# First seven-product block two blocks later, activation sums spread out, conditioning regrouped

## The chip, the core and the metric

The kernel runs on one core of one Trainium2 chip. The engines of the core work side by side and meet only at semaphores: TensorE (PE: matrix products, with PEld for loading the stationary operand), VectorE (DVE), ScalarE (ACT), GpSimd (POOL) and SyncE (SP, which here issues most transfers). Operands lie in on-chip memory in 128 partitions; products are summed in PSUM. The metric is the device time of one launch in microseconds. Before the change three runs took 3255.46, 3265.27 and 3267.32 us; the median, 3265.27 us, is the time to which the change is compared.

## The reference

The input is one sequence of 512 positions with 1024 features. It goes through three layers: two "first" layers (l = 0, 1) and one "second" layer. Each has a feed-forward part (FFN), a mixer (four kinds of attention or recurrence) and another FFN, so there are six FFNs. In the first layers each part is conditioned on a vector `c`:

```python
cond = jax.nn.silu(c)
mod = (cond @ ada_w[l] + ada_b[l]).reshape(B, N_SUBLAYERS, 3, 1, D)   # per part: shift, gain, gate
h = adaln_pre(x, norm_g[l, 0], mod[:, 0, 0], mod[:, 0, 1])            # rms norm, times (1+gain), plus shift
x = x + 0.5 * mod[:, 0, 2] * swiglu(h, ffn1_w13[l], ffn1_w2[l])
def swiglu(h, w13, w2):
    a, b = jnp.split(h @ w13, 2, axis=-1)
    return (jax.nn.silu(a) * b) @ w2                                   # 1024 -> 2816 -> 1024
```

The second layer's FFNs have the same form without conditioning.

## The kernel before

**Precision.** Every matrix product is made of three: a float32 value is split into a high part `hi` (a cast by ACT) and a low part `lo` (value minus `hi`, by DVE), and PE sums hi·hi, hi·lo and lo·hi (`mm3`, lines 308, 311 and 312; line 889 in the seven-product blocks). So each half chunk of weights costs one ACT cast (line 786) and one DVE subtraction (line 787) before PE can use it.

**An FFN** (`ffn`, line 827) makes the 2816 hidden features in 22 blocks (n = 0 to 21) of 128, each with a gate half (`a`) and an up half (`b`). A block is made in one of two ways:

- *plain* (`Q`, `unit_q`): four units of 12 matmuls with 512 columns, 48 in all.
- *seven-product* (`P`, `unit_p`): seven units of 12 matmuls with 256 columns, 84 in all. This form replaces eight half-size products by seven. It needs four sums of weight quarters per block (tiles `S`, line 769, DVE), and sums of activations that are the same for all blocks of the FFN (tiles `e`, made once by `tsums`, line 797).

The units of P are numbered 1, 2, 5, 6, 3, 7 and 4; 1 and 2 (PSUM tiles `A` and `B`) and 3 use the plain activations `hh`, `hl`; the third in order, 5 (PSUM tile `D`), is the first to need a sum of weights and the `e` tiles. Unit 4 of a block is put into the block after it. Which blocks are P is set by the tuple `seven`: twelve blocks from n = 3 in the four FFNs of the first layers, nine odd ones from n = 3 in the two FFNs of the second layer (there `norm` is set). After blocks 6, 14 and 21 the hidden features made so far are multiplied down to the output (units `D`, 16 per slab, the "slabs").

`Units` (line 697) lists all units in order and works five ahead: `take` hands one unit to PE, after `ahead` has loaded, cast and subtracted until five are ready. Hence the order of the program on each engine is the order in which this code issues work; each engine then runs its own list strictly in order, and a scheduler only interleaves neighbours.

**tsums** works in four steps (k = 0 to 3). In each, DVE scales two feature blocks (line 2116), forms four half-width sums and differences (lines 807 and 809) and, after two ACT casts, two low parts (line 824). `ffn` calls one step after each of the units 1 to 4 (`next(ts)`), and `first_block()` after unit 0.

**Conditioning.** 16 modulation vectors of 1024 are made in the background of the FFNs and of the mixers' last product. For each, eight weight chunks of 512 KB are loaded by SP (`ada_load`, line 380), DVE adds chunk times condition to an accumulator `acc` (lines 396 and 398), and then PE transposes `acc` (line 406, eight matmuls) and DVE reduces it to a vector (line 407). `ada_ahead` issues a load if none is waiting in `ada_in`; `bg` runs one step of `mod_steps`. In an FFN the calls stand in alternating units (plain units, the down units, and P blocks with n divisible by 4). Inside an FFN the chunk's tile has one buffer (`bufs=1`).

**Small results.** `snap` copies 128x256 pieces of PSUM to tiles `sn` (five buffers, ACT, line 899); the sum of two of them goes to a tile `c` (line 920, DVE), used in line 924.

**Side work.** `side` is a generator that sets up tables for the mixers, one step after each finished block with n > 2. In the first FFN its first step loads a table on POOL's queue into one of the four weight buffers (line 525), its second multiplies it on PE (line 533).

The lines of the program that the diff touches:

Of the kernel before, what the change touches and what calls it, by code (L numbers as in the profile page):

```python
# [9 lines left out]
F32 = mybir.dt.float32  # L10
F32R = mybir.dt.float32r
AF = mybir.ActivationFunctionType
ALU = mybir.AluOpType
# [6 lines left out]
KD = 8  # L20
# [205 lines left out]
def _body(tc, nc, ctx, I, out):  # L226
# [10 lines left out]
    def nm(s):  # L237
        cnt[0] += 1
        return f"{s}{cnt[0]}"
# [139 lines left out]

    def ada_load(pool):  # L380
        l, k, c0 = ada_src.pop(0)
        raw = pool.tile([128, 1024], F32, tag="raw", bufs=4 if pool is WB else 1, name=nm("raw"))
        nc.sync.dma_start(raw, I["ada"][l, k * 128:(k + 1) * 128, c0:c0 + 1024])
        return raw

    def ada_ahead(pool):

        if ada_src and not ada_in:
            ada_in.append(ada_load(pool))

    def mod_steps(l, s, r):
        acc = P.tile([128, 1024], F32, tag="acc", bufs=1, name=nm("acc"))
        for k in range(KD):
            raw = ada_in.pop(0) if ada_in else ada_load(WB)
            if k == 0:
                i = V.tensor_scalar(acc, raw, cond[:, 0:1], None, op0=ALU.mult)
            else:
                i = V.scalar_tensor_tensor(acc, raw, cond[:, k:k + 1], acc, op0=ALU.mult, op1=ALU.add)  # L398
            dep(i, order["lo"])
            if k < KD - 1:  # L400
                yield
        m = P.tile([128, KD], F32, name=nm("mod"))
        for g in range(2):
            ps = psa()
            for k in range(4):
                PE.transpose(ps[:, k * 128:k * 128 + 128], acc[:, (4 * g + k) * 128:(4 * g + k) * 128 + 128], ident)
            V.tensor_reduce(m[:, 4 * g:4 * g + 4], ps.rearrange("p (k c) -> p k c", k=4), axis=AX.X, op=ALU.add)
        V.tensor_tensor(m, m, C(("adab", l), (3 * s + r) * 8, 8), op=ALU.add)
        if r == 1:
            V.scalar_tensor_tensor(m, m, 1.0, C(("ng", l), s * 8, 8), op0=ALU.add, op1=ALU.mult)  # L410
        elif r == 2 and s != 1:
            V.tensor_scalar(m, m, 0.5, None, op0=ALU.mult)
        mods[l, s, r] = m
        yield

    def all_steps():
        for m in MODS:
# [88 lines left out]
    def bg():  # L506
        next(bg_it, None)
# [319 lines left out]
    def ffn(wa, wd, emit_d, q0=None, side=None, norm=None, operand=None):  # L827
# [3 lines left out]
            yield  # L831
            yield from fr
        table(SILU_SET)
        seven = (3, 5, 7, 9, 11, 13, 15, 17, 19) if norm is not None else (3, 4, 5, 7, 8, 10, 11, 13, 15, 16, 18, 19)
        with tc.tile_pool(name=nm("fp"), bufs=1) as FP:
            f = Units(wa, wd, FP, seven)
            e = [FP.tile([128, 4, 4, 256], F32R, name=nm("e")) for _ in range(2)]
# [40 lines left out]
            def unit_p(n, p, w):  # L878
                S_ = f.acc.setdefault(n, {})
                b = {1: "A", 6: "A", 7: "A", 4: "A", 2: "B", 5: "D", 3: "D"}[p]  # L880
                if p in (1, 2, 5):
                    S_[b] = (psm if b == "B" else psa)(b)
                q = S_[b][:, 0:256]
                k0, t = {1: (0, 0), 2: (4, 0), 3: (4, 1)}.get(p, (None, {5: 0, 6: 1, 7: 2, 4: 3}.get(p)))
                for k in range(4):
                    s = slice(k * 128, k * 128 + 128)
                    xh, xl = (a[:, k, t] if k0 is None else a[:, k0 + k, HV[t]] for a in (e if k0 is None else (hh, hl)))
                    for i, (v, x) in enumerate(((w[0], xh), (w[0], xl), (w[1], xh))):
                        PE.matmul(q, v[:, s], x, start=p in (1, 2, 5) and k + i == 0, stop=k == 3 and i == 2,  # L889
                                  skip_group_check=p not in (1, 2, 5))  # L890

                if n % 4 == 0 and p == 1:
                    ada_ahead(FP)
                elif n % 4 == 0 and p == 3:
                    bg()

                def snap(i):
                    S_[i] = FP.tile([128, 256], F32, tag="sn", bufs=5, name=nm("sn"))
                    S.copy(S_[i], q)
                if p == 1:  # L900
                    snap(1)
                elif p == 2:
                    S_["g"] = FP.tile([128, 512], F32, tag="ga", bufs=2, name=nm("ga"))
                    V.tensor_tensor(S_["g"][:, HV[0]], S_[1], q, op=ALU.add)
                elif p == 5:
                    snap(5)
                elif p == 6:
                    snap(2)
                elif p == 3:
                    g = S_["g"]  # L910
                    V.tensor_tensor(g[:, HV[1]], S_[2], q, op=ALU.add)
                    if norm is not None:
                        V.tensor_tensor(g, g, box["r"], op=ALU.mult)
                    act(g, g, AF.Silu)
                    if norm is not None:
                        V.tensor_tensor(g, g, box["r"], op=ALU.mult)
                elif p == 7:
                    snap(3)
                    S_["c"] = FP.tile([128, 256], F32, tag="c", bufs=2, name=nm("c"))
                    V.tensor_tensor(S_["c"], S_[3], S_[5], op=ALU.add)  # L920
                else:
                    u, g = w_("u"), S_["g"]
                    V.tensor_tensor(u[:, HV[0]], g[:, HV[0]], q, op=ALU.mult)
                    V.tensor_tensor(u[:, HV[1]], g[:, HV[1]], S_["c"], op=ALU.mult)
                    hidden(n, u)
                    del f.acc[n]

# [14 lines left out]
            while f.n[1] < len(f.units):  # L942
                x = f.units[f.n[1]]
                if x[0] == "D" and x[1] == 2 and x[2] == KD - 2:
                    break
                x, w = f.take()
                if x[0] == "D":
                    s, d, h = x[1:]
                    slab, m = SLABS[s], len(SLABS[s]) // 2
                    if (s, d, h) == (2, 0, 0):  # L950
                        table(LN_SET)
                    if h == 0:
                        qd[d] = psa() if d % 2 else psm()
                    mm(qd[d], w, slab[h * m:h * m + m], ALL, h * m, 2 * m)
                    if h:
                        bg()
                    else:
                        ada_ahead(FP)
                    if h and s < 2:
                        emit_d.acc(d, qd[d], s == 0)  # L960
                    elif h:
                        emit_d(d, qd[d], ALL, False)
                else:
                    (unit_q if x[0] == "Q" else unit_p)(x[1], x[2], w)
                if done == 0:
                    first_block()
                elif done < 5:
                    next(ts)
                done += 1
            if ada_in:  # L970
                bg()
            qs, ws = {}, {}
            for d in (KD - 2, KD - 1):
# [1205 lines left out]
```

## Time and profile before

| | before |
|---|---|
| median of three runs | 3265.27 us |
| the profiled execution | 3260.05 us |
| its span, first to last instruction | 3258.3 us |
| mean granted TensorE clock | 0.986 of full |
| PE busy | 3150.6 us (97%) |
| DVE busy | 2228.9 us (68%) |
| ACT busy | 1517.7 us (47%) |
| chain that ended last | PE 83%, DVE 9%, DMA 2%, ACT 2% |

The profile is of one execution. Its busy shares are means over the whole span; a view with a window shows a stretch of it. On PE "idle before" is time in which the engine waited, with the instruction that released it. Matmuls overlap: the distance between the starts of two of them, not the duration of one, is what a matmul costs in a row of many. The four FFNs of the first layers begin their block 1 near 60, 792, 1161 and 1886 us of the span; the two of the second layer lie after 2230 us.

### The profile page before, as it was taken

The page shows a single profiled execution, that of the slowest core. Times are in us where ns is not written, and L with a number is a line of the kernel's source. Part 1 is how long each engine was busy: PE and PEld are TensorE (multiplying, and loading weights), DVE is VectorE, ACT ScalarE, POOL GpSimd, SP SyncE. Part 2 cuts the span into 40 slices and gives each one's busy share as a digit, 9 for nine tenths or more (in the row PEclk, how much of TensorE's full clock was granted, in tenths as well). Part 3 has the DMA queues.
Part 4 walks back from the last instruction along what each step waited for, and adds up shares of the span by engine and source line. Part 5 has one row for each costly group of instructions (what it writes and reads, how often), then busy time and mean ns, then how long its engine had stood idle before and what let it go on. Part 6 is the DMA issues. An engine that isn't in the chain of part 4 may idle for free.

```text
span 3258.3 us, 49205 instructions
## 1 busy us (share of the span) xinstructions
PE 3150.6 (97%) x18436; PEld 2753.0 (84%) x18436; DVE 2228.9 (68%) x4084; ACT 1517.7 (47%) x2953; POOL 422.2 (13%) x492
## 2 busy tenths in 40 slices
PE   7999999999999999999999999999999999999998
PEld 5898877888898888898788898888888788888887
DVE  7787676668887697775766686567566544576664
ACT  4453354553453353343555554345444445664442
POOL 2000132213000210003221311002000210220001
PEclk8999999999999999999999999999999999999999
DMA  6545542114555535543320334234332355433322
GB/s 226 172 155 170 183 136 85 40 50 152 170 160 162 162 112 180 174 151 124 105 75 30 110 101 159 90 123 141 98 110 98 114 171 151 133 122 112 104 96 92
DMA packets 136287, 415.38 MB, mean 127 GB/s; under 512 B 16824, under 2 KB 31036, under 8 KB 135776
## 3 DMA queue, kind: packets, MB, share of 16 engines
q1 hardware_dynamic: 129840, 391.27, 37.6%
q0 software_dynamic: 6064, 20.76, 2.1%
q8 instruction: 145, 2.38, 0.3%
q14 instruction: 94, 0.77, 0.1%
q10 hardware_dynamic: 144, 0.21, 0.0%
HBM read 379.58 MB, written 22.51 MB: 123 GB/s over the span
## 4 chain that ended last, share of the span: by engine, by line
PE 83%; DVE 9%; DMA 2%; ACT 2%; POOL 2%; issue 2%; SPq 0%; DVEq 0%; ACTq 0%; POOLq 0%
PE A L889 11%; PE m L311 10%; PE m L308 10%; PE m L312 10%; PE a L308 7%; PE a L311 7%; PE a L312 7%; PE D L889 6%; PE B L889 3%; PE o L1655 2%; PE pt L1649 1%; DMA raw<-in_ada_dram 1%; DVE lo L297 1%; DVE acc L398 1%; DVE lo L787 1%
## 5 line engine op out<-in xcount | busy, mean ns | idle before, releaser
L786 ACT CAST hi<-raw 128x512 fp32r<-128x512 f32 (+1 forms) x726 | 438.5, 607 | 713.4 <-PE m L311 289.4
L787 DVE TENSOR_TENSOR lo<-raw,hi 128x512 fp32r<-128x512 f32 (+1 forms) x726 | 486.6, 675 | 226.9 <-ACT hi L786 217.1
L308 PE MATMUL m<-hh,hi 128*128 128x512 f32 (+1 forms) x1200 | 467.8, 390 | 11.4 <-ACT hh L483 6.4
L311 PE MATMUL m<-hl,hi 128*128 128x512 f32 (+1 forms) x1200 | 461.4, 385 | 10.6 <-DVE hl L638 8.3
L312 PE MATMUL m<-hh,lo 128*128 128x512 f32 (+1 forms) x1200 | 457.5, 381 | 5.0 <-DVE lo L297 5.0
L889 PE MATMUL A<-e,hi 128*128 128x256 f32 x1584 | 295.7, 285 | 0.1
L297 DVE TENSOR_TENSOR lo<-raw,hi 128x512 fp32r<-128x512 f32 (+1 forms) x264 | 200.2, 769 | 136.9 <-ACT hi L296 129.0
L786 ACT CAST hi<-S 128x512 fp32r<-128x512 f32 x264 | 163.8, 622 | 269.8 <-PE a L311 113.3
L308 PEld LDWEIGHTS m<-hh,hi 128*128 128x128 f32 x1200 | 230.9, 192 | 51.8 <-ACT hh L483 6.5
L311 PEld LDWEIGHTS m<-hl,hi 128*128 128x128 f32 x1200 | 230.7, 192 | 50.7 <-DVE hl L638 10.8
L311 PE MATMUL a<-hl,hi 128*128 128x512 f32 (+1 forms) x736 | 270.4, 367 | 2.4 <-DVE hl L628 2.4
L312 PEld LDWEIGHTS m<-hh,lo 128*128 128x128 f32 x1200 | 230.5, 192 | 47.5 <-DVE lo L297 7.6
L308 PE MATMUL a<-hh,hi 128*128 128x512 f32 (+1 forms) x736 | 269.6, 367 | 0.0
L312 PE MATMUL a<-hh,lo 128*128 128x512 f32 (+1 forms) x736 | 269.1, 366 | 0.0
L296 ACT CAST hi<-raw 128x512 fp32r<-128x512 f32 (+1 forms) x264 | 158.4, 614 | 237.1 <-PE m L311 124.8
L889 PEld LDWEIGHTS A<-e,hi 128*128 128x128 f32 x1584 | 252.1, 194 | 3.9 <-ACT hi L786 0.7
L787 DVE TENSOR_TENSOR lo<-S,hi 128x512 fp32r<-128x512 f32 x264 | 181.1, 688 | 76.5 <-ACT hi L786 76.0
L889 PE MATMUL A<-e,lo 128*128 128x256 f32 x792 | 225.3, 285 | 0.0
L308 PE MATMUL m<-u,hi 128*128 128x512 f32 (+1 forms) x576 | 216.0, 375 | 0.0
L308 PE MATMUL a<-u,hi 128*128 128x512 f32 (+1 forms) x576 | 215.1, 374 | 0.0
L311 PE MATMUL a<-u,hi 128*128 128x512 f32 (+1 forms) x576 | 214.4, 372 | 0.0
L312 PE MATMUL a<-u,lo 128*128 128x512 f32 (+1 forms) x576 | 214.4, 372 | 0.0
(524 smaller groups left out, 7124.5 us busy)
## 6 DMA issues: line engine op xcount, KB each, us to landing
raw<-in_ada_dram SPq DMA_DIRECT2D x144, 512.0 KB, 4.1
raw<-in_f1a_dram SPq DMA_DIRECT2D x88, 512.0 KB, 4.3
raw<-in_f2a_dram SPq DMA_DIRECT2D x88, 512.0 KB, 3.8
raw<-in_win_dram SPq DMA_DIRECT2D x48, 512.0 KB, 3.6
raw<-in_g1a_dram SPq DMA_DIRECT2D x44, 512.0 KB, 3.5
raw<-in_g2a_dram SPq DMA_DIRECT2D x44, 512.0 KB, 3.4
raw<-in_f1b_dram SPq DMA_DIRECT2D x32, 512.0 KB, 3.9
raw<-in_f2b_dram SPq DMA_DIRECT2D x32, 512.0 KB, 3.6
```

The lines of the kernel that those rows point to most:

```text
L296: order["hi"] = S.copy(h, raw[:, s])
L297: order["lo"] = V.tensor_tensor(l, raw[:, s], h.bitcast(F32), op=ALU.subtract)
L308: i = PE.matmul(o, wh, xh, start=start, stop=False)
L311: PE.matmul(o, wh, xl, start=False, stop=False)
L312: j = PE.matmul(o, wl, xh, start=False, stop=stop)
L398: i = V.scalar_tensor_tensor(acc, raw, cond[:, k:k + 1], acc, op0=ALU.mult, op1=ALU.add)
L786: order["hi"] = S.copy(h, src)
L787: order["lo"] = V.tensor_tensor(l, src, h.bitcast(F32), op=ALU.subtract)
L889: PE.matmul(q, v[:, s], x, start=p in (1, 2, 5) and k + i == 0, stop=k == 3 and i == 2, skip_group_check=p not in (1, 2, 5))
L1649: PE.transpose(pt[:, j * 128:j * 128 + 128], t[:, j * 128:j * 128 + 128], ident)
L1655: PE.matmul(o, r[:, j * 128:j * 128 + 128], v, start=j == 0, stop=j == len(vs) - 1)
```

## The change

Six things change in the code.

1. `seven`: in the four FFNs of the first layers still twelve P blocks, now 5, 7, 8, 9, 11, 12, 13, 15, 16, 17, 19 and 20 (blocks 3 and 4 become plain); in the second layer's two FFNs block 3 becomes plain, eight P blocks are left.
2. `tsums`: its four steps follow units 1, 4, 7 and 10 instead of 1, 2, 3 and 4.
3. The conditioning chunk has two buffers inside an FFN, and `ada_ahead` may hold two.
4. `mod_steps` yields after its eighth chunk too, so that transposes and reduction stand in the next step, together with the next vector's first chunk; there is no yield after the reduction.
5. In P blocks the calls stand at n = 5, 8, 12, 13, 16 and 20; the last slab's units from d = 4 on load nothing new.
6. `sn` has four buffers instead of five, and the tile `c` is gone: the sum overwrites `S_[3]`.

```diff
     def ada_load(pool):
         l, k, c0 = ada_src.pop(0)
-        raw = pool.tile([128, 1024], F32, tag="raw", bufs=4 if pool is WB else 1, name=nm("raw"))
+        raw = pool.tile([128, 1024], F32, tag="raw", bufs=4 if pool is WB else 2, name=nm("raw"))
...
     def ada_ahead(pool):
-        if ada_src and not ada_in:
+        if ada_src and len(ada_in) < (1 if pool is WB else 2):
             ada_in.append(ada_load(pool))
     def mod_steps(l, s, r):
...
             dep(i, order["lo"])
-            if k < KD - 1:
-                yield
+            yield
         m = P.tile([128, KD], F32, name=nm("mod"))
...
         mods[l, s, r] = m
-        yield
...
-        seven = (3, 5, 7, 9, 11, 13, 15, 17, 19) if norm is not None else (3, 4, 5, 7, 8, 10, 11, 13, 15, 16, 18, 19)
+        seven = (5, 7, 9, 11, 13, 15, 17, 19) if norm is not None else (5, 7, 8, 9, 11, 12, 13, 15, 16, 17, 19, 20)
...
-                if n % 4 == 0 and p == 1:
+                if n in (5, 8, 12, 13, 16, 20) and p == 1:
                     ada_ahead(FP)
-                elif n % 4 == 0 and p == 3:
+                elif n in (5, 8, 12, 13, 16, 20) and p == 3:
                     bg()
                 def snap(i):
-                    S_[i] = FP.tile([128, 256], F32, tag="sn", bufs=5, name=nm("sn"))
+                    S_[i] = FP.tile([128, 256], F32, tag="sn", bufs=4, name=nm("sn"))
...
                     snap(3)
-                    S_["c"] = FP.tile([128, 256], F32, tag="c", bufs=2, name=nm("c"))
-                    V.tensor_tensor(S_["c"], S_[3], S_[5], op=ALU.add)
+                    V.tensor_tensor(S_[3], S_[3], S_[5], op=ALU.add)
...
-                    V.tensor_tensor(u[:, HV[1]], g[:, HV[1]], S_["c"], op=ALU.mult)
+                    V.tensor_tensor(u[:, HV[1]], g[:, HV[1]], S_[3], op=ALU.mult)
...
-                    if h:
+                    if s == 2 and d > 3:
+                        if ada_in:
+                            bg()
+                    elif h:
                         bg()
...
-                elif done < 5:
+                elif done in (1, 4, 7, 10):
                     next(ts)
                 done += 1
-            if ada_in:
+            while ada_in:
                 bg()
```

**Place 1, DVE, first FFN, up to the first sums of weights.** `lo` is a low part of weights, `e61` the low activation sums, `acc85` the conditioning accumulator, `u` hidden features, `S` sums of weights. Before:

```order
L824 TENSOR_TENSOR e61_387<-t116_572,e60_386 128x512
L398 SCALAR_TENSOR_TENSOR acc85_458<-raw113_568,cond_97,acc85_458 128x1024
L824 TENSOR_TENSOR e61_387<-t117_573,e60_386 128x512
L769 TENSOR_TENSOR S120_601<-raw75_414 128x512
L853 TENSOR_TENSOR u128_640<-u128_640,a123_607 128x512
L769 TENSOR_TENSOR S125_622<-S120_601,raw70_404 128x512
L787 TENSOR_TENSOR lo122_604<-S120_601,hi121_603 128x512
```

After:

```order
L822 TENSOR_TENSOR e61_387<-t140_693,e60_386 128x512
L851 TENSOR_TENSOR u144_721<-u144_721,a136_676 128x512
L822 TENSOR_TENSOR e61_387<-t141_694,e60_386 128x512
L398 SCALAR_TENSOR_TENSOR acc85_458<-raw137_689,cond_97,acc85_458 128x1024
L842 TENSOR_TENSOR u146_725<-u144_721,u145_724 128x512
L785 TENSOR_TENSOR lo150_734<-raw112_573,hi149_733 128x512
L785 TENSOR_TENSOR lo154_753<-raw112_573,hi153_752 128x512
L398 SCALAR_TENSOR_TENSOR acc85_458<-raw152_750,cond_97,acc85_458 128x1024
L767 TENSOR_TENSOR S155_769<-raw126_632 128x512
```

Before, the first sum of weights stands right behind the last activation sum, with the second plain block's features after it. Now it stands behind the third block's features; between the start of the first plain block's rows and it, DVE has two plain blocks' rows and four conditioning steps more.

**Place 2, DVE, first FFN, the end of the first modulation vector.** `acc85` gets its eighth chunk, `a` is the PSUM tile of the transposes, `mod` the vector, and line 1040 (before) adds the first down product with it. Before:

```order
L398 SCALAR_TENSOR_TENSOR acc85_458<-raw252_1203,cond_97,acc85_458 128x1024
L844 TENSOR_TENSOR u247_1182<-u245_1178,u246_1181 128x512
L787 TENSOR_TENSOR lo260_1238<-raw230_1099,hi259_1237 128x384
L787 TENSOR_TENSOR lo264_1254<-raw230_1099,hi263_1253 128x384
L407 TENSOR_REDUCE mod255_1219<-a256_1220 128x4
```

After:

```order
L398 SCALAR_TENSOR_TENSOR acc85_458<-raw159_788,cond_97,acc85_458 128x1024
L785 TENSOR_TENSOR lo171_827<-S169_824,hi170_826 128x512
L851 TENSOR_TENSOR u163_808<-u163_808,a158_775 128x512
...
L785 TENSOR_TENSOR lo197_947<-raw148_731,hi196_946 128x512
L909 TENSOR_TENSOR ga179_866<-sn187_905,D183_874 128x256
L406 TENSOR_REDUCE mod191_925<-a192_926 128x4
```

The reduction stood four rows behind the eighth chunk, with the transposes of PE between them; now it stands twelve rows behind, and in block 5 instead of the first slab.

**Place 3, SP, first FFN, the first transfers.** `in_ada` is a conditioning chunk, `in_f1a` a chunk of weights. Before:

```order
L745 DMA raw91_476<-in_f1a_dram 128x1024
L383 DMA raw95_495<-in_ada_dram 128x1024
L745 DMA raw109_549<-in_f1a_dram 128x1024
L383 DMA raw113_568<-in_ada_dram 128x1024
L383 DMA raw124_620<-in_ada_dram 128x1024
L383 DMA raw160_788<-in_ada_dram 128x1024
L745 DMA raw141_690<-in_f1a_dram 128x1024
```

After:

```order
L743 DMA raw126_632<-in_f1a_dram 128x1024
L383 DMA raw137_689<-in_ada_dram 128x1024
L743 DMA raw133_670<-in_f1a_dram 128x1024
L383 DMA raw152_750<-in_ada_dram 128x1024
L383 DMA raw159_788<-in_ada_dram 128x1024
L383 DMA raw173_843<-in_ada_dram 128x1024
L535 DMA nsa_r_103<-ng167_816 4x128
L383 DMA raw202_982<-in_ada_dram 128x1024
```

Both lists have three or more conditioning chunks in a row ahead of a weight chunk; the new one carries twice as many chunks in the same number of plain units.

## Rows read from the trace of the kernel before

**Rows 1.** The page's first part: busy time, share of the span, instructions.

```profile
PE 3150.6 (97%) x18436; PEld 2753.0 (84%) x18436; DVE 2228.9 (68%) x4084; ACT 1517.7 (47%) x2953; POOL 422.2 (13%) x492
```

**Rows 2.** Waits of PE, whole span: total us, times, longest us.

```profile
PE D L889 <- ACT hi L786: 9.8, 6, 2.7
PE a L406 <- DVE acc L398: 6.3, 3, 2.5
```

**Rows 3.** Timeline of PE, first FFN: start, duration, idle before and releaser.

```profile
70.91 0.39 PE L308 MATMUL m<-hh,hi 128*128 128x512 f32 x1
...
81.79 0.28 PE L889 MATMUL A<-hh,hi 128*128 128x256 f32 x1
...
87.72 0.80 PE L889 MATMUL D<-e,hi 128*128 128x256 f32 x2 [2.65 <-ACT hi L786]
88.82 0.58 PE L889 MATMUL D<-e,lo 128*128 128x256 f32 x1 [0.30 <-DVE lo L787]
...
94.86 0.38 PE L889 MATMUL D<-hh,hi 128*128 128x256 f32 x1 [0.55 <-ACT hi L786]
...
99.33 0.28 PE L889 MATMUL B<-hh,hi 128*128 128x256 f32 x1
```

**Rows 4.** Timeline of PE, second to fourth FFN, same places.

```profile
813.33 0.28 PE L889 MATMUL A<-hh,hi 128*128 128x256 f32 x1
...
829.94 0.28 PE L889 MATMUL B<-hh,hi 128*128 128x256 f32 x1
...
1182.76 0.28 PE L889 MATMUL A<-hh,hi 128*128 128x256 f32 x1
...
1199.78 0.28 PE L889 MATMUL B<-hh,hi 128*128 128x256 f32 x1
...
1907.42 0.28 PE L889 MATMUL A<-hh,hi 128*128 128x256 f32 x1
...
1918.77 0.28 PE L889 MATMUL B<-hh,hi 128*128 128x256 f32 x1
```

**Rows 5.** Windows: us, busy of PE, PEld, DVE, ACT, POOL, PEclk, DMA, GB/s.

```profile
60.00:84.80 24.80, 24.80 (x121) 20.83 (x119) 24.59 (x46) 11.52 (x21) 0.00 (x0) 1.00 0.41 140
...
90.00:92.50 2.50, 2.50 (x14) 2.50 (x13) 2.50 (x4) 0.37 (x1) 0.00 (x0) 0.50 0.14 25
```

**Rows 6.** Chain of waits, first FFN: start, us on the chain, work.

```profile
71.25 0.60 DVE lo L787
...
74.06 1.20 DVE acc L398
...
86.36 0.60 DVE S L769
...
102.37 2.88 PE A L889 x24
```

**Rows 7.** Timeline of PE at the transposes, 130 to 146 and 740 to 775.

```profile
137.97 1.31 PE L406 MATMUL a<-km,acc 128*128 128x128 f32 x8 [2.19 <-DVE acc L398]
...
759.00 1.06 PE L406 MATMUL a<-km,acc 128*128 128x128 f32 x8 [2.54 <-DVE acc L398]
```

**Rows 8.** Windows behind these two.

```profile
138.00:142.50 4.50, 4.50 (x17) 3.78 (x18) 3.79 (x9) 0.00 (x0) 0.00 (x0) 0.62 0.66 204
759.80:763.30 3.50, 3.50 (x20) 3.50 (x19) 3.30 (x5) 0.00 (x0) 2.81 (x2) 0.52 0.77 257
```

**Rows 9.** Groups of DVE instructions: busy, mean ns, idle before and releaser.

```profile
L398 DVE SCALAR_TENSOR_TENSOR acc<-raw,cond,acc 128x1024 f32<-128x1024 f32 x112 | 148.1, 1323 | 67.8 <-DMA raw<-in_ada_dram 67.7
```

**Rows 10.** Window over the pair of P blocks 15 and 16, first FFN.

```profile
296.00:316.00 20.00, 20.00 (x162) 19.73 (x161) 15.10 (x26) 11.05 (x23) 0.00 (x0) 1.00 0.38 118
```

**Rows 11.** Timeline of DVE and of ACT, same pair: a sum, a later snap.

```profile
307.60 0.42 DVE L920 TENSOR_TENSOR c<-sn,sn 128x256 f32<-128x256 f32 x1
...
311.18 0.37 ACT L899 COPY sn<-D 128x256 f32<-128x256 f32 x1
```

## The prediction

> **What bounds the kernel now.** I read the page's busy shares first, then PE's waits, then PE's timeline where the waits lie, then the windows and the chain of waits there, and last the groups of DVE.
>
> PE is busy 97% of the span [rows 1], so only two things can move the time much: PE's own matmuls and the stretches in which it stands. Two of PE's waits belong to lines that the change touches: 9.8 us in six waits of tile D for ACT's `hi`, and 6.3 us in three waits of the transposes for `acc` [rows 2].
>
> The first is the third unit of block 3, the first P block of an FFN. Its neighbourhood must be read as a distance, because matmuls overlap. From the first `A` row of block 3 to the first `B` row of block 4 PE has seven units, 84 matmuls of 256 columns. At full clock 24 such matmuls take 2.88 us of the chain [rows 6], 0.12 us each, so the 84 should take 10.08 us. They take 99.33 − 81.79 = 17.54 us in the first FFN [rows 3] and 16.61, 17.02 and 11.35 us in the next three [rows 4]. The losses are 7.46, 6.53, 6.94 and 1.27 us, together 22.2 us. That is more than the waits: after the wait of 2.65 us the granted clock is 0.50 [rows 5], the lower of the two levels, and the next matmuls cost nearly twice as much.
>
> Why PE waits there: DVE. It is busy 24.59 of 24.80 us from the first plain block on [rows 5], with four `tsums` steps pressed into four units, and its first sum of weights starts only at 86.36 [rows 6]. ACT casts that sum, and unit 5 of block 3 starts at 87.72 [rows 3]. Without a wait it would have started two units (2 × 1.44 us) after 81.79, at 84.67: it is 3.05 us late.
>
> **First P block at n = 5.** Two plain blocks now stand ahead of it. One plain block takes PE 81.79 − 70.91 = 10.88 us [rows 3], so PE comes to that unit 21.76 us later. DVE gets more to do before its first sum of weights, as place 1 of the order shows: eight low parts and four feature operations of the same size at 0.60 us, and four conditioning steps at 1.20 us [rows 6], 4.8 + 2.4 + 4.8 = 12.0 us. The lateness of 3.05 us turns into a lead of 21.76 − 12.0 − 3.05 = 6.7 us. Against this: a conditioning step also waits for its chunk, 67.7 us over 112 steps [rows 9], 0.6 us each, 2.4 us for four more. A lead of 4.3 us stays. So I take the whole 22.2 us off. Bounds: nothing (the wait moves to block 5 as it is) to 22.2 us. The twelve P blocks of the first layers' FFNs stay twelve, so their matmuls don't change.
>
> **tsums spread out.** The same DVE rows, no more and no fewer. Their results are needed only in block 5's third unit; unit 10, after which the last step is issued, lies eight units ahead of it. What is late if they were: the same D row, so it has the bounds above.
>
> **Second layer.** Block 3 turns from P to plain in two FFNs: 10.88 − 10.08 = 0.80 us of PE each, +1.6 us. PE is the bound there, nothing hides it. All six waits of D [rows 2] lie in the first layers' FFNs, so the later start gains nothing here.
>
> The Trainium skill, page "TensorE: Matmul & The Clock Gate", section "Back-to-back issue gap", gives 262 cycles for 256 columns and 518 for 512 at 2.4 GHz, that is 109 and 216 ns. By it the swap would cost 48 × 0.216 − 84 × 0.109 = 1.2 us a block, 2.4 us in both, an estimate that speaks a little more against the change. The trace has 120 ns for 256 columns and 10.88 / 48 = 227 ns for 512, both slower than the page, and it is the short form that loses more by it.
>
> **Transposes a step later.** Place 2 of the order: the reduction stands twelve DVE rows behind the eighth chunk instead of four, and a whole background step lies between, so PE finds `acc` done. This takes away the 6.3 us [rows 2]. Two of the three waits were followed by a low clock: 0.62 over 4.5 us and 0.52 over 3.5 us [rows 8], which is 4.5 × 0.38 + 3.5 × 0.48 = 3.4 us of lost PE time. Together 9.7 us. One of the two, the 2.54 us at 759 [rows 7], is in the mixer's last product, where DVE and POOL finish the residual and its statistics for the next FFN; PE's earlier finish can be given back to them. No row settles this; of its 2.54 + 1.68 = 4.2 us I take half. So 9.7 − 2.1 = 7.6 us, with bounds 0 and 9.7. The shift costs nothing in due times: the one vector that was finished just in time before (the first gate, in the first slab) now has its eighth chunk in block 4.
>
> **Two chunks ahead.** Calls of `ada_ahead` and `bg` alternate in every part of an FFN, so `ada_in` never holds two and the new limit isn't reached; only the second buffer works. It lets SP issue a chunk before DVE is done with the last one. This shortens the 67.7 us that DVE waits [rows 9], but PE doesn't wait for that beyond the rows counted, so it gains nothing by itself. The cost could be on SP's queue, which is in order: place 3 shows three chunks in a row ahead of a weight chunk. PE needs that one in block 6, a whole P block later. I take 0; the bound is one more stall like block 3's, 7 us. The same 0, with the same bound, goes for the POOL load and the small product of the side work, which now come right ahead of block 5.
>
> **Fewer small buffers.** The sum in place is ready 0.42 us after 307.60, and the next snap into the buffer that it frees comes at 311.18 [rows 11]: 3.2 us in hand. Price 0 while DVE is less than that behind.
>
> **The sum.** −22.2 − 7.6 + 1.6 = −28.2 us on the profiled execution's 3260.05 us: 3231.9 us. That execution lies 5.2 us under the median of the three runs, 3265.27; carried over, 3237 us.
>
> **Rivals.**
>
> *The stall moves to block 5.* DVE comes to its first sum more than 6.7 us later than counted, because chunks are late or ACT's casts hold it. For: the lead is a difference of two large terms, and eight conditioning steps now fall into the first four plain blocks instead of four. Against: the chunk waits in the mean take 2.4 us of it. The three large losses stay, and only 1.27 + 7.6 − 1.6 = 7.3 us are gained: 3252.8 on the profiled execution, 3258 as a median. No change that can be told.
>
> *The transposes' part is worth nothing,* given back at the next wait each time: −22.2 + 1.6 = −20.6 us, 3245 as a median. Still faster. That two chunks are never ahead points this way for the conditioning part as a whole; that the three waits are PE's own points against it.
>
> *Rows of three P blocks run DVE dry: slower.* Blocks 7 to 9, 11 to 13 and 15 to 17 stand in a row, where before there were pairs (and one row of three, ahead of which PE had stood anyway). A P block costs DVE seven low parts, four sums and one feature low part at 0.60 us and five half-width operations of at most 0.42 us [rows 6, 11], 7.2 + 2.1 = 9.3 us of 10.08; with a conditioning step 10.5. Blocks 12 and 13 both have one: 3 × 9.3 + 2 × 1.2 = 30.3 us of DVE for 30.24 of PE. From the point where this lag eats the five units worked ahead (5 × 1.44 = 7.2 us), each row of three would cost a stall like block 3's, 7 us. In the three FFNs with conditioning there are nine: +63 us, 3295 on the profiled execution, 3300 as a median; four of them undo the gain. Against it: over the pair 15 and 16, with one step, DVE is busy 15.1 of 20 us [rows 10], because part of the sums is done ahead, and the lag at the triple's end is near zero by the count.
>
> **How the numbers follow.** My forecast 0.53, the transposes worth nothing 0.19, the stall moved 0.19, the triples 0.09. A change under 0.5%, 16 us, can't be told from none here: the three runs alone span 12 us. Faster by over 0.5% (under 3249 us) are the first two cases, less a little for a stall that stays in one FFN: 0.70. Within 0.5%: 0.21. Slower: 0.09. The range goes from 3226 us (all 30.3 us taken, runs a few us low) to 3262 us (the moved stall and a few us of scatter); beyond lie the triples and little else.
>
> **What would show it.** Right: the distance from the first `A` to the next block's `B` is 10.1 us at block 5 in all four FFNs, with a granted clock of 1.00; no wait of the transposes for `acc`; the second layer's FFNs 0.8 us longer each. Wrong: waits of D for `hi` still near 10 us, now at block 5; or new waits of `A`, `B` or `D` for `hi` or `lo` in blocks 9, 13 and 17; or a larger wait of the statistics (`st`) for POOL after the mixer, which would show the transposes' gain given back.

## The result, and the profile after

The changed kernel takes 3229.74 us, the median of four runs (3226.64 to 3232.60), beside 3263.22 us of the kernel before in the same set: a ratio of 0.990, 95% interval 0.9878 to 0.9922. The forecast was 3237 us. The profiled executions go from 3260.05 to 3226.64 us, 33.4 us less where 28.2 were counted.

The page's first part answers to [rows 1]:

```profile
PE 3141.0 (97%) x18364; PEld 2745.4 (85%) x18364; DVE 2223.4 (69%) x4062; ACT 1512.1 (47%) x2939; POOL 423.5 (13%) x492
```

PE's busy time fell by 9.6 us (3150.6 to 3141.0), and the span less that busy time from 107.7 to 83.9 us, by 23.8: together the 33.4. The first part is mostly time at the lower clock: the mean granted clock rose from 0.986 to 0.989, which is 3258.3 × 0.014 − 3224.9 × 0.011, some 10 us.

PE's largest waits (total us, times, longest):

```profile
PE st L588 <- POOL st L591: 13.6, 9, 3.1
PE m L311 <- DVE hl L636: 6.1, 10, 1.5
PE a L429 <- ACT sq L428: 5.9, 1, 5.9
PE m L308 <- ACT hh L481: 5.4, 2, 4.1
```

Both rows of [rows 2] are gone: no line of the whole list is a wait of `D`, `A` or `B`, and none is one of the transposes (line numbers are one or two smaller now in the part that the diff touches: `D` is L887, the transposes are L405). The wait for POOL's statistics grew from 12.3 to 13.6 us.

PE's timeline at the first P block, block 5, in the four FFNs of the first layers: the first `D` row, and the first `m` row behind the block's late unit.

```profile
107.25 0.40 PE L887 MATMUL D<-e,hi 128*128 128x256 f32 x2
111.57 1.04 PE L405 MATMUL a<-km,acc 128*128 128x128 f32 x8
118.05 0.40 PE L308 MATMUL m<-hh,hi 128*128 128x512 f32 x1
...
823.95 0.40 PE L887 MATMUL D<-e,hi 128*128 128x256 f32 x2
833.89 0.40 PE L308 MATMUL m<-hh,hi 128*128 128x512 f32 x1
...
1186.75 0.40 PE L887 MATMUL D<-e,hi 128*128 128x256 f32 x2
1196.69 0.40 PE L308 MATMUL m<-hh,hi 128*128 128x512 f32 x1
...
1899.64 0.40 PE L887 MATMUL D<-e,hi 128*128 128x256 f32 x2
1909.58 0.40 PE L308 MATMUL m<-hh,hi 128*128 128x512 f32 x1
```

Block 6 is plain, so the distance that the forecast named, from block 5's `A` to the next block's `B`, does not exist; it was a slip. From `D` on there are five short units and one plain one, 60 × 0.12 + 12 × 0.227 = 9.92 us. The rows have 9.94 us three times, and 10.80 in the first FFN, where eight transposes stand between. Nothing is lost there.

How far DVE and ACT are ahead is read on ACT's timeline, at the first cast of a sum of weights in the first FFN:

```profile
99.56 1.35 ACT L784 CAST hi<-S 128x512 fp32r<-128x512 f32 x2 [0.98 <-DVE S L767]
```

The first of the two ends at 100.2 us, 7.1 us ahead of the `D` row that needs it (107.25). Read the same way, the other three FFNs have 6.8, 4.9 and 9.9 us. The forecast said 4.3 to 6.7.

The windows that answer to [rows 5], the plain blocks of FFN 1 and then block 5 of the four FFNs:

```profile
60.00:104.20 44.20, 44.20 (x194) 35.69 (x192) 43.52 (x72) 19.42 (x34) 0.71 (x1) 1.00 0.58 190
104.20:118.10 13.90, 13.90 (x106) 13.35 (x106) 10.42 (x21) 7.44 (x15) 2.11 (x4) 1.00 0.90 297
821.00:834.00 13.00, 13.00 (x100) 12.51 (x98) 10.65 (x21) 6.47 (x13) 0.00 (x0) 1.00 0.61 199
1184.00:1197.00 13.00, 13.00 (x99) 12.47 (x98) 11.43 (x19) 6.95 (x15) 0.00 (x0) 1.00 0.61 204
1896.80:1910.00 13.20, 13.20 (x99) 12.67 (x98) 8.33 (x15) 7.35 (x15) 0.00 (x0) 1.00 0.31 92
```

DVE is still full over four plain blocks (43.52 of 44.20 us), but nobody waits for it, and the clock is 1.00. The group of DVE that answers to [rows 9]:

```profile
L398 DVE SCALAR_TENSOR_TENSOR acc<-raw,cond,acc 128x1024 f32<-128x1024 f32 x112 | 150.2, 1341 | 0.2 <-DMA raw<-in_ada_dram 0.2
```

Its 67.7 us of waiting for chunks are 0.2 now.

The program is cut best at the first `st` matmul of each norm, which ends a part. On PE's timeline of the changed kernel:

```profile
398.96 0.59 PE L588 MATMUL st<-st,ones 128*128 128x256 f32 x2
...
752.49 0.48 PE L588 MATMUL st<-st,ones 128*128 128x256 f32 x1 [1.31 <-POOL st L591]
...
1114.77 0.59 PE L588 MATMUL st<-st,ones 128*128 128x256 f32 x2
...
1477.55 0.59 PE L588 MATMUL st<-st,ones 128*128 128x256 f32 x2
```

The same marks before are 410.82, 767.14, 1136.30 and 1507.93 us. Lengths of the parts between such marks, in the profiled executions (us; the kernels below the second row are those of the experiments):

| | FFN 1 and start | mixer 1 | FFN 2 | FFN 3 | mixer 2 | FFN 4 | FFN 5 | mixer 3 | FFN 6 |
|---|---|---|---|---|---|---|---|---|---|
| before | 410.8 | 356.3 | 369.2 | 371.6 | 352.7 | 362.3 | 355.3 | 289.7 | 367.4 |
| changed | 399.0 | 353.5 | 362.3 | 362.8 | 351.7 | 359.8 | 356.1 | 289.4 | 367.7 |
| place alone | 412.2 | 354.7 | 378.4 | 369.2 | 352.4 | 359.8 | 356.2 | 288.6 | 367.7 |
| transposes alone | 412.4 | 356.1 | 370.3 | 368.4 | 353.9 | 362.3 | 356.9 | 291.6 | 367.4 |
| buffer alone | 406.9 | 356.9 | 367.7 | 369.6 | 353.4 | 361.3 | 356.6 | 290.1 | 367.4 |
| place and transposes | 405.0 | 355.9 | 368.4 | 364.3 | 355.3 | 360.8 | 356.1 | 291.6 | 367.7 |
| place and buffer | 399.9 | 355.5 | 364.2 | 366.3 | 352.9 | 359.8 | 356.1 | 289.2 | 367.7 |
| triples in layer 2 | 399.7 | 355.1 | 362.6 | 361.9 | 353.5 | 360.8 | 352.8 | 288.2 | 364.4 |

The last row is the changed kernel up to FFN 4, word for word; so two executions of one program differ by up to 1.7 us in a part, and no smaller difference is read from one trace.

### The profile page after: what moved, and what is told of

Same layout as the page of the kernel before. It is cut to its first block, busy times and chain, and to the rows that moved or that the text cites. A ratio compares the mean times of both kernels' runs of the same rounds, so it can differ in the third digit from the quotient of the medians.

```text
span 3224.9 us, 49124 instructions
## 1 busy us (share of the span) xinstructions
PE 3141.0 (97%) x18364; PEld 2745.4 (85%) x18364; DVE 2223.4 (69%) x4062; ACT 1512.1 (47%) x2939; POOL 423.5 (13%) x492
## 4 chain that ended last, share of the span: by engine, by line
PE 88%; DVE 5%; POOL 2%; ACT 2%; DMA 1%; issue 1%; SPq 0%; DVEq 0%; ACTq 0%; POOLq 0%
PE A L887 11%; PE m L311 11%; PE m L308 11%; PE m L312 11%; PE a L311 8%; PE a L312 8%; PE a L308 8%; PE D L887 6%; PE B L887 3%; PE o L1655 2%; PE pt L1649 1%; DVE lo L297 1%; PE a L1423 1%; PE a L1439 1%; DVE x L2091 1%
## 5 line engine op out<-in xcount | busy, mean ns | idle before, releaser
L785 DVE TENSOR_TENSOR lo<-raw,hi 128x512 fp32r<-128x512 f32 (+1 forms) x728 | 492.2, 679 | 235.7 <-ACT hi L784 228.1
L297 DVE TENSOR_TENSOR lo<-raw,hi 128x512 fp32r<-128x512 f32 (+1 forms) x264 | 201.9, 776 | 134.4 <-ACT hi L296 126.6
L887 PE MATMUL A<-e,hi 128*128 128x256 f32 x1536 | 283.5, 283 | 0.0
L311 PE MATMUL a<-hl,hi 128*128 128x512 f32 (+1 forms) x752 | 277.3, 369 | 2.4 <-DVE hl L626 2.4
L312 PE MATMUL a<-hh,lo 128*128 128x512 f32 (+1 forms) x752 | 275.9, 367 | 0.0
L887 PEld LDWEIGHTS A<-e,hi 128*128 128x128 f32 x1536 | 241.8, 192 | 2.8
L887 PE MATMUL A<-e,lo 128*128 128x256 f32 x768 | 217.3, 283 | 0.0
L312 PE MATMUL m<-u,lo 128*128 128x512 f32 (+1 forms) x576 | 214.3, 372 | 0.0
```

What stands on the lines that cost most here:

```text
L297: order["lo"] = V.tensor_tensor(l, raw[:, s], h.bitcast(F32), op=ALU.subtract)
L311: PE.matmul(o, wh, xl, start=False, stop=False)
L312: j = PE.matmul(o, wl, xh, start=False, stop=stop)
L785: order["lo"] = V.tensor_tensor(l, src, h.bitcast(F32), op=ALU.subtract)
```

## The experiments

Each was timed beside the kernel before on the same chip. Kernels with the same number under "before there" ran in one set; kernels of different sets are compared by their distance to before, which is 33.5 us for the changed kernel.

| kernel | median us | before there | ratio, 95% |
|---|---|---|---|
| place alone | 3263.42 | 3264.42 | 0.9992 to 1.0010 |
| transposes alone | 3263.70 | 3264.42 | 0.9989 to 1.0008 |
| buffer alone | 3257.95 | 3264.42 | 0.9973 to 0.9990 |
| changed, first P at 3 | 3255.91 | 3264.42 | 0.9966 to 0.9983 |
| changed, one buffer | 3235.10 | 3265.62 | 0.9892 to 0.9922 |
| changed, transposes back | 3230.46 | 3265.62 | 0.9879 to 0.9912 |
| changed, sums packed | 3230.53 | 3265.62 | 0.9881 to 0.9910 |
| changed, more P blocks at 3 and 4 | 3239.61 | 3265.62 | 0.9907 to 0.9937 |
| place and buffer | 3236.67 | 3264.97 | 0.9901 to 0.9928 |
| place and transposes | 3246.35 | 3264.97 | 0.9928 to 0.9953 |
| triples in layer 2 | 3225.21 | 3264.97 | 0.9863 to 0.9893 |
| longer rows | 3228.78 | 3264.97 | 0.9872 to 0.9899 |

### The place alone

In the kernel before, only the tuple:

```diff
-        seven = (3, 5, 7, 9, 11, 13, 15, 17, 19) if norm is not None else (3, 4, 5, 7, 8, 10, 11, 13, 15, 16, 18, 19)
+        seven = (5, 7, 9, 11, 13, 15, 17, 19) if norm is not None else (5, 7, 8, 9, 11, 12, 13, 15, 16, 17, 19, 20)
```

> The kernel before with the new tuple `seven` alone (first P block at 5; the sums of activations still after units 1 to 4, one chunk buffer, transposes where they were). Theory A (the place): PE stands at the first P block because DVE comes too late to its first sum of weights, and two plain blocks ahead cure that: 22.2 us less, 1.6 us more in the second layer, so about 20.6 us under the kernel before; no wait of D for `hi`, about 6 us of transposes waiting for `acc` stay. Theory B (the chunks): what makes DVE late is its waiting for conditioning chunks with one buffer (67.7 us before), so the stall only moves to block 5: D waits of 7 us or more, time within 5 us of before.

Measured: nothing gained. The waits of `D` are gone as the first theory has it, but another took their place. PE's waits:

```profile
PE a L406 <- DVE acc L398: 22.3, 5, 8.4
PE st L590 <- POOL st L593: 14.6, 9, 3.1
PE m L311 <- DVE hl L638: 6.6, 10, 1.5
```

How it comes about is read on three timelines of the first FFN. DVE adds the seventh chunk, then the eighth:

```profile
106.42 1.28 DVE L398 SCALAR_TENSOR_TENSOR acc<-raw,cond,acc 128x1024 f32<-128x1024 f32 x1 [2.55 <-DMA raw<-in_ada_dram]
...
111.24 1.28 DVE L398 SCALAR_TENSOR_TENSOR acc<-raw,cond,acc 128x1024 f32<-128x1024 f32 x1 [1.73 <-DMA raw<-in_ada_dram]
```

SP issues the eighth chunk only when the seventh has left the one buffer (106.42 + 1.28 = 107.70 us):

```profile
107.74 0.33 SPq L383 DMA_DIRECT2D raw<-in_ada_dram  x1
```

And PE stands with the transposes, which come right behind the eighth chunk:

```profile
112.58 1.97 PE L406 MATMUL a<-km,acc 128*128 128x128 f32 x8 [6.85 <-DVE acc L398]
```

So with one buffer a chunk can't be fetched while the last one is in use, and PE, with no stall in front of it any more, runs into that. In FFN 2 the same wait is 8.4 us long. Two more waits of 2.2 and 1.6 us, for low parts of weights, lie in FFN 3; they come up again under "Open".

### The transposes alone, the buffer alone

In the kernel before, `yield` after every chunk and none after the reduction:

```diff
-            if k < KD - 1:
-                yield
+            yield
```

> The kernel before with the shifted yield alone (transposes and reduction a background step later). Forecast: 7.6 us less, 9.7 if nothing is given back; D waits for `hi` stay near 9.8 us, no wait of the transposes for `acc`. Rival (given back at the next wait): within 2 us of before, and the statistics' wait for POOL (12.3 us before) grows by about as much as was taken away.

Measured: nothing gained. PE's waits, and its timeline at the first vector:

```profile
PE st L588 <- POOL st L591: 15.3, 10, 3.1
PE D L887 <- ACT hi L784: 10.0, 6, 2.6
...
PE a L405 <- DVE acc L398: 2.6, 1, 2.6
```

```profile
138.52 1.46 PE L405 MATMUL a<-km,acc 128*128 128x128 f32 x8 [2.59 <-DVE acc L398]
```

The first vector's transposes still wait, and where they stood before [rows 7]: the first slab needs this vector, so the step that was meant to come later is run at once. The waits at 759 and 1260 us are gone, but POOL's statistics are waited for 3.0 us longer (12.3 to 15.3). Most of that is one new wait right behind the first of the two, at the end of mixer 1:

```profile
768.44 0.70 PE L588 MATMUL st<-st,ones 128*128 128x256 f32 x2 [2.25 <-POOL st L591]
```

Of the 2.54 us taken away there 2.25 come back, and the mixer takes 356.1 us beside 356.3.

The second buffer, with the smaller `sn` and without `c`, which make room for it:

```diff
-        raw = pool.tile([128, 1024], F32, tag="raw", bufs=4 if pool is WB else 1, name=nm("raw"))
+        raw = pool.tile([128, 1024], F32, tag="raw", bufs=4 if pool is WB else 2, name=nm("raw"))
```

> The kernel before with two chunk buffers inside an FFN, a limit of two, and the small buffers of the change (four `sn`, no tile `c`), which make room for it; `seven`, the sums and the transposes as before. Theory A (the place): DVE's 67.7 us of waits for chunks go, but the D waits for `hi` stay at 8 us or more, and the time is within 3 us of before. Theory B (the chunks): DVE is pulled forward, the D waits fall under 3 us, and 15 to 22 us are gained.

Measured: 6.5 us less, between the two theories. PE's waits:

```profile
PE D L889 <- ACT hi L786: 9.8, 6, 2.7
...
PE a L406 <- DVE acc L398: 2.6, 1, 2.6
```

```profile
755.66 1.07 PE L406 MATMUL a<-km,acc 128*128 128x128 f32 x8 [2.63 <-DVE acc L398]
```

The chunk waits of DVE are gone from its list, and yet `D` waits its 9.8 us as in [rows 2]: the chunks don't hold up the first P block. They did hold up the transposes, 6.3 us before and 2.6 now: the waits at 138 and 1260 us, inside FFNs, are gone, and the one at the end of mixer 1 is left, where a chunk goes to one of the four weight buffers in all kernels.

### The changed kernel with the first P block back at 3

```diff
-        seven = (5, 7, 9, 11, 13, 15, 17, 19) if norm is not None else (5, 7, 8, 9, 11, 12, 13, 15, 16, 17, 19, 20)
+        seven = (5, 7, 9, 11, 13, 15, 17, 19) if norm is not None else (3, 4, 7, 8, 9, 11, 12, 13, 15, 16, 17, 19)
...
-                elif done in (1, 4, 7, 10):
+                elif done in (1, 3, 5, 7):
```

> The changed kernel with the first P block of the first layers' FFNs back at 3 (3, 4, 7, 8, 9, 11, 12, 13, 15, 16, 17, 19: twelve again); sums of activations after units 1, 3, 5 and 7, since block 3 needs them; two buffers and the later transposes stay. In the changed kernel the cast of the first weight sum ends 7.1, 6.8, 4.9 and 9.9 us ahead of its first D matmul in the four FFNs. Theory A (the place): two plain blocks fewer take 21.76 us of PE away and 12.0 us of DVE, so the lead becomes -2.7, -3.0, -4.9 and +0.1 us: D waits of about 2.7, 3.0 and 4.9 us in three FFNs and a clock of 0.50 behind them, 18 to 25 us slower than the changed kernel. Theory B (the chunks) or C (the spread sums): no D wait over 1 us, and the time is the changed kernel's within 3 us.

Measured: 8.5 us under before, so 25 us less than the changed kernel gains, as the first theory has it. But `D` waits for another cast than was expected:

```profile
PE D L887 <- ACT e L821: 10.8, 4, 3.4
```

It waits for the last activation sums, which this kernel makes later than the one before. So the run shows that block 3 is too early for what lies ahead of it, not that the lead for weights is the one computed.

### Undoing one part of the changed kernel

One buffer and a limit of one:

> The changed kernel with one chunk buffer inside an FFN and the limit of one. After the first four runs: the place alone gained nothing, since 22.3 us of transposes waiting for `acc` came for the 9.8 us of D waiting for `hi`; there DVE stood for chunks until just before the transposes. Theory D (one chain): with one buffer a chunk is fetched only when DVE is done with the last, so the conditioning runs late, and wherever PE needs something behind it, PE stands. Then the buffer is needed here as well: 10 to 25 us slower than the changed kernel, with waits of the transposes for `acc` (L405) of 5 us or more and DVE's chunk waits over 60 us. Theory A as on record (the second buffer is worth 0, the later transposes keep PE clear of the chunks): within 3 us of the changed kernel.

Measured: 30.5 us under before, and 4.6 us slower than the next two kernels, which ran on the same chip: in between. The intervals overlap (the table), so that this loss is more than scatter is likely, not shown. DVE's chunk waits are back, with little of it passed on to the transposes (1.6 us, once):

```profile
DVE acc L398 <- DMA raw<-in_ada_dram: 76.3, 59, 3.1
```

Transposes right behind the eighth chunk:

> The changed kernel with transposes and reduction right behind the eighth chunk again. Theory A as on record: 7.6 us slower (9.7 at most), with about 6 us of L405 or its like waiting for `acc`. Theory D (one chain): with two buffers the eighth chunk is there in time, so about 3 us of `acc` waits as in the run with the buffer alone (2.6 us there), plus the clock behind them: 2 to 6 us slower.

Measured: 3230.46 us, the changed kernel's time within the scatter. No wait of the transposes is in PE's list. With two buffers the later step buys nothing.

Sums of activations after units 1 to 4:

> The changed kernel with the sums of activations after units 1 to 4 again, as before. Theory A as on record: their results are needed only in block 5, so within 3 us of the changed kernel, no new wait of PE. Rival C (the spread counts): DVE, busy nearly 100% in blocks 1 and 2, is late with low parts or with `u`, PE waits for `lo` or D for `hi`, 5 us slower or more.

Measured: 3230.53 us, the changed kernel's time within the scatter, and no wait of `D`.

### Two parts together

> The kernel before with the new `seven` and the second chunk buffer (limit two, four `sn`, no `c`); sums still after units 1 to 4, transposes right behind the eighth chunk, the calls in P blocks at n divisible by 4. Alone the place gained nothing and the buffer about 6.5 us. Theory D (one chain: where the place alone stalls, PE waits for transposes that wait for a chunk fetched late): the buffer takes that away, so the D waits and the `acc` waits are both gone, and at least 25 us are gained, 3230 to 3240 us. Theory C (the spread sums or the later transposes are needed too): `acc` waits of 5 us or more stay, 3245 us or more.

Measured: 28.3 us under before. The waits of `D` are gone and the transposes wait once, 1.2 us. PE's list begins

```profile
PE st L590 <- POOL st L593: 14.0, 9, 3.1
PE m L308 <- ACT hh L483: 7.4, 2, 6.1
PE m L311 <- DVE hl L638: 6.2, 10, 1.5
```

> The kernel before with the new `seven` and the later transposes; one chunk buffer, sums after units 1 to 4, calls in P blocks at n divisible by 4. Each of the two edits gained nothing alone. Theory D (one chain): the step between the eighth chunk and its transposes gives the late chunk time, as in the run with one buffer (3235 us), so 22 to 30 us are gained, with chunk waits of DVE near 75 us that cost PE nothing. Theory C (spread sums or the added calls at 5 and 13 are needed too): `acc` waits of 5 us or more, 3250 us or more.

Measured: 18.6 us under before, less than expected. PE's list has

```profile
PE a L405 <- DVE acc L398: 6.0, 3, 3.3
```

The later step is a weaker remedy than the buffer for the same late chunk.

### Is there more in the place?

One P block more in each FFN:

> The changed kernel with one P block more in every FFN: block 4 in the four of the first layers (13 in all), block 3 in the two of the second layer (9, its sums after units 1, 3, 5 and 7). Each such block takes 10.08 instead of 10.88 us of PE: 6 x 0.80 = 4.8 us less, if DVE is in time. By the leads measured at block 5 (7.1, 6.8, 4.9 and 9.9 us) less one plain block of 10.88 us of PE plus some 6 us of DVE work that then lies behind: 2.2, 1.9, 0.0 and 5.0 us at block 4, so no D wait over 0.5 us: 4.8 us faster than the changed kernel. Rival: the lead shrinks by a whole block, PE stands 3 to 6 us with a low clock behind it in three FFNs: 8 to 15 us slower.

Measured: 9 us slower than the two kernels above on the same chip, but hardly for the rival's reason: the first cast of a sum of weights is 10.4 us or more ahead at block 4 and 2.3 to 5.0 at block 5, and `D` waits 0.3 us in the first FFN. My count of the lead, by a block's PE time less a block's DVE work, does not hold here. FFN 2 alone is 4.3 us longer (366.6 beside 362.3). On PE's timeline, behind the norm's statistics at 756.33:

```profile
763.94 1.09 PE L405 MATMUL a<-km,acc 128*128 128x128 f32 x8 [0.74 <-DVE acc L398]
767.56 0.39 PE L308 MATMUL m<-hh,hi 128*128 128x256 f32 x1 [2.52 <-ACT hh L625]
```

A modulation vector is still being made there, and the normalised features wait for it; in the changed kernel its transposes stand at 744.40, ahead of the statistics. I read it so: a plain block gives the conditioning two calls, a P block one or none, and with a plain block fewer the vector isn't ready; no run tried more calls there. In the second layer block 3 as P made FFN 5 and 6 0.8 and 0.9 us longer instead of shorter: in FFN 5 `D` waits 0.8 us for the last activation sums, in FFN 6 PE waits 0.9 us for a low part.

> The changed kernel with twelve P blocks, the same as in the first layers, in the second layer's two FFNs too (5, 7, 8, 9, 11, 12, 13, 15, 16, 17, 19, 20 for the eight odd ones). There the cast of the first weight sum is 8.4 to 10.4 us ahead of its matmul, and in the first layers, with conditioning on DVE as well, a second and third P block in a row hold a lead of 6.5 us. If rows of P don't run DVE dry: 8 x 0.80 = 6.4 us less than the changed kernel, leads of about 6.5 us. Rival (DVE runs dry; `norm` costs DVE more per block): D, A or B wait for `hi` or `lo`, no gain or slower.

```diff
-        seven = (5, 7, 9, 11, 13, 15, 17, 19) if norm is not None else (5, 7, 8, 9, 11, 12, 13, 15, 16, 17, 19, 20)
+        seven = (5, 7, 8, 9, 11, 12, 13, 15, 16, 17, 19, 20)
```

Measured: 3225.21 us, 39.8 us under before, 6.3 more than the changed kernel and the most of all here. FFN 5 and 6 are 3.3 us shorter each (the table of parts), 3.2 by the count, and the leads in their rows of three are 6.4 to 10.4 us. That is 0.83 us a block. By the cycle table of the Trainium skill, page "TensorE: Matmul & The Clock Gate", section "Back-to-back issue gap", which the page gives for a matmul by itself and not for a row of them, the estimate is 1.2 us a block, as in the prediction. The trace doesn't agree, and the measured 0.83 us decides.

> The same, with two more P blocks, 10 and 18, in each FFN of the first layers (rows 7 to 13 and 15 to 20; conditioning called in 10 and 18 too): another 8 x 0.80 = 6.4 us, 12.8 us under the changed kernel, if the lead of 6.5 us of the third P block in a row holds through seven. By a count of 9.3 us of DVE a P block and 1.2 a step it just does: 7 x 9.3 + 4 x 1.2 = 69.9 us of DVE for 70.6 of PE. Rival (DVE runs dry in the long row, the forecast's last rival): the lead falls from block to block, PE stands for `hi` or `lo` in blocks 11 to 13, and the time is above that of the run with triples in the second layer.

Measured: 3228.78 us, nothing gained over the kernel above. In the first three FFNs the lead in the long rows stays at 4.8 us or more; in FFN 4 it falls to 0.5, 0.1 and 2.0 us in the first row:

```profile
PE D L887 <- ACT hi L784: 1.2, 1, 1.2
PE D L887 <- DVE lo L785: 1.0, 1, 1.0
```

DVE was not short of time there, as the rival has it: it is busy 5.57 of the 10 us from 1990 on, and stands 4.3 us for a chunk of weights.

```profile
1996.68 0.69 DVE L767 TENSOR_TENSOR S<-raw 128x512 f32<-128x512 f32 x1 [4.33 <-DMA raw<-in_f2a_dram]
```

FFN 4 is 2.9 us longer (363.7 beside 360.8), FFN 2 2.6 us with a hurried vector as above, and mixer 3, whose code is the same, 5.9 us. There PE stands 4.1 us longer than in the kernel above, most of it for small transfers (`two`), and the mean granted clock is 0.983 beside 0.988; why the transfers come later isn't shown.

## Why the prediction was right, and where it was not

By parts of the profiled executions, counted as the forecast did (transposes at 138, 759 and 1260 us put to FFN 1, mixer 1 and FFN 3):

| part | forecast | measured |
|---|---|---|
| FFN 1: 7.46 + 2.19 + 1.7 | −11.4 | −11.9 |
| mixer 1: half of 4.2 | −2.1 | −2.8 |
| FFN 2 | −6.5 | −6.9 |
| FFN 3: 6.94 + 1.6 | −8.5 | −8.9 |
| mixer 2 | 0 | −0.9 |
| FFN 4 | −1.3 | −2.4 |
| FFN 5, FFN 6 | +1.6 | +1.1 |
| mixer 3 and the end | 0 | −0.7 |

Each part came within 1.2 us. The 5 us over the forecast are small differences of one sign in all parts, each no larger than what two executions of one program differ by. The parts came out because the waits were counted right; which edit takes which wait away was not, and that the total is so near owes something to luck: 7.6 us were counted for an edit that gives almost nothing, and nothing for the second buffer, which gives 6.5.

**First P block at 5.** Right in what it takes away (22.2 us counted, all `D` waits gone) and in the lead (4.3 to 6.7 us, measured 4.9 to 9.9). Wrong in that it stood as a term of its own: alone it gained 1.0 us, which is within the scatter. With the second buffer it is worth 28.3 − 6.5 = 21.8 us, with the later transposes 18.6 − 0.7 = 17.9; 20.6 were counted, the 1.6 us of the second layer taken off.

**Two chunks ahead.** This is the step that failed: "PE doesn't wait for that beyond the rows counted, so it gains nothing by itself". The second buffer gains 6.5 us alone, and without it the changed kernel is some 4.6 us slower, with intervals that overlap. Two of the three waits for `acc` of [rows 2], at 138 and 1260 us, were waits for the chunk behind it, read as the transposes' own.

**Transposes a step later.** Mis-sized: 7.6 us counted, 0.7 measured alone and nothing as the last part added. Of the three waits that were counted under it the buffer takes two away, and nearly all of what the third gives comes back. It does its work only where the chunk is late: beside the place alone it is worth 17.6 us (18.6 − 1.0). That some is given back at the mixer's end, half by the forecast, holds in kind; the sign that it named for this, a larger wait of `st` for POOL, is there. How much is not settled: with the later transposes alone nearly all; in the changed kernel `st` waits 1.31 us at 752.49, where it waited for nothing before, and the part gains 2.8 of 4.2 us; in the other execution of the same program it waits 2.34 us, and the part gains 1.2.

```profile
754.80 0.70 PE L588 MATMUL st<-st,ones 128*128 128x256 f32 x2 [2.34 <-POOL st L591]
```

**Sums spread out and second layer.** For the spread 0 counted, and no difference measured; +0.8 us counted for FFN 5 and FFN 6 each, +0.8 and +0.3 measured. For the small buffers 0 counted, and no wait of PE for `sn` is in the changed kernel's list.

**Rivals.** The stall did move to block 5 in the kernel with neither the buffer nor the later step, but only in its first two FFNs, and as a wait for a chunk, not for a cast of weights. Rows of three did not run DVE dry: in the changed kernel the lead is 6.4 us or more in every block of them.

**Open.** The forecast's sum has no term for the calls at n = 5 and 13 and for the last slab, and the forecast gives no reason for that. From the place with the buffer (28.3 us) to the changed kernel with the transposes back (35.2 us) there are 7 us that lie in these calls, the last slab or the spread sums. From the place with the later transposes (18.6 us) to the changed kernel with one buffer (30.5 us) there are 12 in the same edits and the smaller `sn`. The spread alone is worth nothing beside the rest; that it is the calls was not tried by itself.

Some 4 of the 7 us can be seen in FFN 3 (366.3 us beside 361.9 in the changed kernel with the transposes back). With the place and the buffer PE takes the gate halves of two blocks there in a row, 48 `m` matmuls, ahead of the first one's up half, and waits twice for low parts:

```profile
1162.42 0.50 PE L312 MATMUL m<-hh,lo 128*128 128x512 f32 x1 [2.12 <-DVE lo L787]
1167.07 0.50 PE L312 MATMUL m<-hh,lo 128*128 128x512 f32 x1 [1.64 <-DVE lo L787]
```

The place alone has the same order and the same two waits; the other kernels in the table of parts have neither. Which of the edits sets this order isn't shown.

## What to carry to other kernels

Where one engine is late for several consumers, the edits that cure each wait are not terms of a sum: with one cured, the bound engine runs into the next, and the time stays. Follow a wait back to its last releaser (here the wait for `acc` to a transfer held up by a single buffer) before giving its price to the edit that only moves the waiting instruction. And before a form of a block is changed, count what else is paced by it, as the conditioning calls are here.

## What was not expected of the hardware

Two executions with the same instructions up to FFN 4 differ by 0.4 to 1.7 us in a part, mostly but not always with the same one ahead, and by 4.5 us at its end (2189.12 and 2193.57 us). A term under 2 us is therefore not settled by one trace.
